# A mixture-of-experts stage: the eighth row block of the gate and up matrices as one fp32 product instead of three split ones

## The chip, the cores and the metric

The kernel runs on one core of a Trainium2 chip. The core's engines work side by side and meet through semaphores: TensorE (PE in the profile, with its weight loads as PEld), VectorE (DVE), ScalarE (ACT), GpSimd (POOL), and SyncE (SP), which here only issues DMA transfers. The metric is the device time of one execution in microseconds (us); the median of several runs counts, and lower is better.

## The reference, cut to what matters

A two-layer encoder on 512 tokens of width 1024, in float32. Each layer has a token mixer (attention of two kinds) and a mixture of experts. Only the experts matter here: a router picks two of 16 experts for each token, and each expert is a SwiGLU block with an inner width of 256.

```python
hg = jnp.einsum('td,edf->tef', t, w_gate)     # w_gate: (16, 1024, 256) per layer
hu = jnp.einsum('td,edf->tef', t, w_up)
act = jax.nn.silu(hg) * hu * combine[..., None].astype(t.dtype)
y = jnp.einsum('tef,efd->td', act, w_down)    # w_down: (16, 256, 1024)
```

`combine` is zero for the experts that a token did not choose, so the kernel computes each expert for its own tokens only.

## The kernel before, in words

**Split products.** A float32 product on PE takes several passes over the moving operand. The kernel replaces most of them by a product of two rounded parts: an operand z is split into H, z rounded to the type fp32r, and L, the rest z - H, also fp32r. Three fp32r matmuls, H·H, H·L and L·H, then stand for one float32 product. ACT writes H (a copy with a change of type) and DVE writes L (a subtraction). `wsplit` (lines 197 to 220; ACT at line 217, DVE at line 218) does this for a weight matrix, in pieces of 512 columns; `split_ps` (lines 341 to 343) for a tile that stands in PSUM; and `gemm3` (lines 222 to 229) issues the three matmuls of each 128-row block k, at lines 227, 228 and 229.

**One expert** (lines 1129 to 1210). At most 128 tokens go to an expert. `x_load` gathers their rows from DRAM into `xe` (line 1133, an indirect DMA issued by POOL). `x_split` transposes the eight 128x128 blocks of `xe` on PE, four at a time into one PSUM tile, and splits them into `xH` and `xL` (lines 342 and 343). `x_prod` splits one weight matrix of 1024x256, held as eight row blocks of 256 columns, in four pieces of two blocks, and multiplies: eight blocks times three matmuls of 256 columns, all added up in one PSUM tile `mm`. `x_gate` does this for the gate matrix and applies SiLU (ACT, line 1159); `x_up` does it for the up matrix, multiplies both results (DVE, line 1166, tile `ea`) and splits a part of the down matrix. `x_down` transposes `ea` to `eT` (ACT, line 1186), and multiplies it with the down matrix at line 1203: of its four blocks of 128 rows and 512 columns, two are split and two go unsplit as float32 products that read the raw tile (group `mm<-raw,eT`). DVE scales the result with a row (`ye`, line 1204), and POOL adds it to `xsum` in DRAM with an indirect DMA (line 1208, a scatter-add). The last two experts of a layer skip the scatter; their results stay in SBUF (`yk`).

**The order.** The loop over experts calls gate(e), down(e-1), up(e) and the split for e+1 in turn. A framework orders the instructions on each engine by priority and by its own estimate of time, and sets the semaphores; each engine then works its list in order. Split pieces go through a ring of six buffers for H and six for L (`NWH = 6`), ten pieces per expert. Raw weights, 1 MB each, go through nine buffers (five `e8` and four `raw`), so a load waits until the matrix three experts earlier is through; those of the first four experts are issued ahead of the stage. All weight loads are issued by SP, in order (line 194 for most).

**The end of a layer.** When the last scatter-add has landed, SP loads `xsum` back (line 1336, `xs`), and behind it the first block of the next layer's `w_in`. PE then adds up `xs` and the two kept experts (lines 1343 and 1360, tile `y`).

**Other tiles that the change touches.** `mhalf` is a constant tile of -0.5, of which `pool_rsqrt` uses up to ten columns. `oc`, `code`, `sh` and `sg` are tiles of `overflow`, a branch for an expert with more than 128 tokens.

```python
H = wp.tile([P, h] + shape[1:], F32R, tag="wH", name="wH", bufs=NWH)
L = wp.tile([P, h] + shape[1:], F32R, tag="wL", name="wL", bufs=NWH)
...
ACT.copy(H, raw(s))
V.tensor_sub(L, raw(s), H.bitcast(F32))
...
PE.matmul(o, lhsT=lH, rhs=rH, start=(i == 0), stop=False)
PE.matmul(o, lhsT=lH, rhs=rL, start=False, stop=False)
PE.matmul(o, lhsT=lL, rhs=rH, start=False, stop=(i == n - 1))
```

The lines of code above are cut from `wsplit` and `gemm3`; the functions follow with their line numbers.

Of the kernel before, what the change touches and what calls it, by code (L numbers as in the profile page):

```python
# [8 lines left out]
F32 = mybir.dt.float32  # L9
F32R = mybir.dt.float32r  # L10
BF16 = mybir.dt.bfloat16
I32 = mybir.dt.int32
# [6 lines left out]
P = 128  # L19
S = 512  # L20
D = 1024
NT = S // P
DEPTH = 2
HD = 64
NE = 16
# [10 lines left out]
def constants():  # L36

    parts = []
    off = [0]

    def add(name, a):
        a = np.asarray(a, np.float32).reshape(P, -1)
        _COLS[name] = (off[0], a.shape[1])
        off[0] += a.shape[1]
        parts.append(a)

    p = np.arange(P)
    add("ident", np.eye(P))
    add("tri", (p[:, None] < p[None, :]))
    row = np.repeat(np.arange(S // 64), 64).astype(np.float32)  # L50
    col = np.tile(np.arange(64), S // 64).astype(np.float32)
    inv = (10000.0 ** (-np.arange(0, 32, 2, dtype=np.float64) / 32)).astype(np.float32)
    ang = np.concatenate([row[:, None] * inv, col[:, None] * inv], -1).astype(np.float64)
    cos = np.repeat(np.cos(ang), 2, axis=-1)
    sin = np.repeat(np.sin(ang), 2, axis=-1)
    sin[:, 0::2] *= -1.0
    add("cos", cos.reshape(NT, P, HD).transpose(1, 0, 2))
    add("sin", sin.reshape(NT, P, HD).transpose(1, 0, 2))
    slope = np.exp2(-8.0 * np.arange(1, 13) / 12).astype(np.float32)

    def bias(g, dist, valid):
        b = -slope[4 * g:4 * g + 4, None, None] * dist[None].astype(np.float32)
        b = np.where(valid[None], b, np.float32(NEG))
        return b[[0, 2, 1, 3]].transpose(1, 0, 2)

    d0 = np.abs(np.arange(256)[None, :] - 64 - p[:, None])
    add("bias0", bias(0, d0, d0 <= 64))
    d1 = np.abs(p[None, :] - p[:, None])
    add("bias1", bias(1, 4 * d1, d1 <= 64))
    add("bias2", bias(2, 4 * d1, d1 % 4 == 0))  # L70
    enc = np.zeros((P, NT, 2))
    for t in range(NT):
        enc[:, t, 0] = 128 * (NT - 1 - t)
        enc[:, t, 1] = 128 - p
    add("enc", enc)
    add("iota", np.tile(p, (P, 1)))
    sel = np.zeros((P, 2, P))
    for i in range(8):
        sel[i, i % 2, (i % 4 // 2) * 64:(i % 4 // 2) * 64 + 64] = 1.0
    add("sel", sel)  # L80
    add("mhalf", np.full((P, 16), -0.5))
    return np.ascontiguousarray(np.concatenate(parts, 1))


def build(tc, A, out):
    nc = tc.nc
    with ExitStack() as es:
# [11 lines left out]
        V, ACT, PE, PO, SY = nc.vector, nc.scalar, nc.tensor, nc.gpsimd, nc.sync  # L99
# [7 lines left out]
        def sc(name, shape, dt=F32, p=P):  # L107
            return sp.tile([p] + list(shape), dt, tag="sc", name=name)

        def small(name, shape, dt=F32, bufs=4, p=P):  # L110
            return sm.tile([p] + list(shape), dt, tag=name, name=name, bufs=bufs)
# [85 lines left out]
        def wsplit(src, shape, big=False, tag="raw", behind=()):  # L197

            raw = src if callable(src) else wraw(src, shape, tag)
            a = shape[0]  # L200
            h = 512 // shape[1] if shape[1] < 512 else 1
            hs = []
            if big:
                h = a // 2
                Hb = e8("wHb", shape, F32R)
                Lb = e8("wLb", shape, F32R)
            for i in range(a // h):
                s = slice(i * h, (i + 1) * h)
                if big:
                    H, L = Hb[:, s], Lb[:, s]  # L210
                else:
                    H = wp.tile([P, h] + shape[1:], F32R, tag="wH", name="wH", bufs=NWH)
                    L = wp.tile([P, h] + shape[1:], F32R, tag="wL", name="wL", bufs=NWH)
                with ExitStack() as order:
                    for z in behind:
                        order.enter_context(tc.issue_after(z.ins))
                    ACT.copy(H, raw(s))  # L217
                    V.tensor_sub(L, raw(s), H.bitcast(F32))  # L218
                hs.append((H, L))
            return lambda k, c: tuple(z[:, k % h, c] for z in hs[k // h])  # L220

        def gemm3(o, ks, lf, rf):
            n = len(ks)
            for i, k in enumerate(ks):
                lH, lL = lf(k)
                rH, rL = rf(k)
                PE.matmul(o, lhsT=lH, rhs=rH, start=(i == 0), stop=False)  # L227
                PE.matmul(o, lhsT=lH, rhs=rL, start=False, stop=False)  # L228
                PE.matmul(o, lhsT=lL, rhs=rH, start=False, stop=(i == n - 1))  # L229

        def row_load(src):
            r = rp.tile([P, D], F32, tag="row", name="row")
# [108 lines left out]
        def split_ps(p, H, L):  # L341
            ACT.copy(H, p)  # L342
            return V.tensor_sub(L, p, H.bitcast(F32))  # L343
# [79 lines left out]
        def layer(l, hH, hL, W0, after=None, qk=None):  # L423
# [586 lines left out]
            def x_src(e, w):  # L1010
                if (e, w) in PRE:
                    return PRE.pop((e, w))
                a = A["w_exp_" + w][l, e]
                return a.rearrange("(k p) n -> p k n", p=P) if w == "down" else a.rearrange("(p k) n -> p k n", p=P)
# [123 lines left out]
            def x_split(e):  # L1138
                xe = XE.pop(e)
                xH = f4("xH", [8, P], F32R)  # L1140
                xL = f4("xL", [8, P], F32R)
                for q in range(2):
                    p = ptp([P, 4, P])
                    transposes(lambda i: xe[:, (4 * q + i) * P:(4 * q + i + 1) * P], p, 4)
                    i = split_ps(p, xH[:, 4 * q:4 * q + 4, :], xL[:, 4 * q:4 * q + 4, :])
                XS[e] = xH, xL
                return i

            def x_prod(e, w):
                xH, xL = XS[e]  # L1150
                W = wsplit(x_src(e, w), x_shape(w), tag=tags.get((e, w)), behind=[order1] if (e, w) in BEHIND else [])
                p = pmm([P, 256])
                gemm3(p, range(8), lambda k: (xH[:, k, :], xL[:, k, :]), lambda k: W(k, slice(0, 256)))
                return p

            def x_gate(e):
# [70 lines left out]
            def overflow():  # L1227
# [3 lines left out]
                with tc.If(rv > CAP):  # L1231
                    token_weights()
                    row = rt("row", [2, NT])
                    V.tensor_scalar(row, sv[:, 0], float(CAP), None, op0=OP.is_ge)
                    code = rt("code", [NT])
                    V.tensor_add(code, enc[:, :, 0], enc[:, :, 1])
                    ow = sc("ow", [2, NT, NE])
                    V.tensor_mul(ow, tmp, row[:, :, :, None].to_broadcast([P, 2, NT, NE]))
                    V.tensor_mul(row, row, code[:, None].to_broadcast([P, 2, NT]))
                    oc = sc("oc", [2, NT, NE])  # L1240
                    V.tensor_mul(oc, o12, row[:, :, :, None].to_broadcast([P, 2, NT, NE]))
                    V.tensor_add(oc[:, 0], oc[:, 0], oc[:, 1])
                    oi = sc("oi", [NE * NT], I32)
                    V.tensor_scalar(oi.rearrange("p (e t) -> p t e", t=NT), oc[:, 0], -1.0, float(S), op0=OP.mult, op1=OP.add)
                    og = sc("og", [NE * NT])
                    V.tensor_add(og.rearrange("p (e t) -> p t e", t=NT), ow[:, 0], ow[:, 1])
                    sh = sc("sh", [NE * NT], I32)
                    sg = rt("sg", [NE * NT])
                    with tc.For_i(0, NE, 1) as e:
                        def blocks(w, tags, view):  # L1250
                            r = []
# [177 lines left out]
```

## Time and profile before

| What | Value |
|---|---|
| Median of three runs | 1363.2 us (1360.3 to 1363.39) |
| Profiled execution, its own time | 1365.39 us |
| Span in its trace | 1363.6 us |
| PE busy, share of the span | 1269.8 us, 93% |
| DVE busy | 1015.7 us, 74% |
| ACT busy | 712.3 us, 52% |
| Granted TensorE clock, mean | 0.975 of full speed |
| DMA moved | 259.37 MB, mean 190 GB/s |

The experts' stage of layer 0 lies at about 500 to 675 us of the span, that of layer 1 at about 1162 to 1336 us. A group of instructions in the profile is named by its line, its engine and its tiles (out<-in); "x512" is a count, and two times behind a bar are the sum of busy time in us and the mean of one in ns. Matmuls are pipelined: the recorded duration of one is longer than the distance to the next, so what a matmul costs in a row of them is the distance between starts. The idle time in brackets is that of the engine just before the instruction, with what ended it.

### The profile page before, as it was taken

How to read it: one execution, taken by the hardware profiler on the slowest of the kernel's cores; microseconds unless marked ns; L12 is line 12 of the kernel's file. 1: busy time of each engine (PE TensorE's matmuls, PEld its weight loads, DVE VectorE, ACT ScalarE, POOL GpSimd, SP SyncE). 2: the span in 40 equal slices, each digit the busy share in tenths (PEclk: the TensorE clock that was granted, in tenths of full speed). 3: DMA queues.
4: the chain of work that ended last, by engine and by line, in shares of the span. 5: the costliest groups of instructions: out<-in, count | busy, mean ns of one | idle time of the engine just before them, and what ended most of it. 6: DMA issues, size and time to landing. Idle time of an engine off the chain costs nothing.

```text
span 1363.6 us, 21396 instructions
## 1 busy us (share of the span) xinstructions
PE 1269.8 (93%) x7967; PEld 1031.1 (76%) x7971; DVE 1015.7 (74%) x2064; ACT 712.3 (52%) x1476; POOL 145.5 (11%) x122
## 2 busy tenths in 40 slices
PE   5899999999999959999889999999999995899997
PEld 4788777778778948888658777777777795788883
DVE  5888778766378879999587887564235878799986
ACT  2344444554744157777445445456555513777770
POOL 1031000000000012222111300000000001223210
PEclk9999999999999969999989999999999997999999
DMA  9745555346165178999553455121214534889963
GB/s 319 230 140 169 185 186 184 126 155 210 38 201 217 63 276 327 313 342 330 177 186 129 155 186 186 63 62 63 63 47 141 192 131 171 322 300 352 335 187 153
DMA packets 124221, 259.37 MB, mean 190 GB/s; under 512 B 18009, under 2 KB 67577, under 8 KB 116176
## 3 DMA queue, kind: packets, MB, share of 16 engines
q1 hardware_dynamic: 102672, 225.46, 46.6%
q0 software_dynamic: 9184, 15.69, 4.9%
q10 hardware_dynamic: 12256, 16.80, 3.9%
q8 instruction: 64, 1.05, 0.3%
q14 instruction: 45, 0.37, 0.1%
HBM read 246.57 MB, written 27.30 MB: 201 GB/s over the span
## 4 chain that ended last, share of the span: by engine, by line
PE 39%; DVE 14%; ACT 4%; DMA 3%; issue 3%; POOL 1%; SPq 0%; ACTq 0%; POOLq 0%; DVEq 0%
DVE wL L218 8%; PE mm L229 6%; PE mm L228 6%; PE mm L227 6%; PE mm L1203 6%; PE tp L335 3%; PE y L1343 2%; PE av L664 1%; ACT wH L217 1%; DMA xr<-xdr 1%; PE y L1360 1%; DMA raw<-in_w_in 1%; ACT eT L1186 1%; DMA xe<-h2d,tidx 1%; DVE ea L1166 1%
## 5 line engine op out<-in xcount | busy, mean ns | idle before, releaser
L218 DVE TENSOR_TENSOR wL<-raw,wH 128x512 fp32r<-128x512 f32 x520 | 340.4, 686 | 95.5 <-ACT wH L217 85.1
L217 ACT CAST wH<-raw 128x512 fp32r<-128x512 f32 x520 | 318.8, 622 | 159.6 <-PE mm L1203 45.7
L227 PE MATMUL mm<-hH,wH 128*128 128x512 f32 x544 | 218.8, 402 | 0.0
L228 PE MATMUL mm<-hL,wH 128*128 128x512 f32 x544 | 216.9, 399 | 0.0
L229 PE MATMUL mm<-hH,wL 128*128 128x512 f32 x544 | 215.8, 397 | 0.0
L227 PE MATMUL mm<-wH,xH 128*128 128x256 f32 x512 | 148.0, 289 | 0.5 <-ACT xH L342 0.5
L229 PE MATMUL mm<-wH,xL 128*128 128x256 f32 x512 | 147.0, 288 | 0.5 <-DVE xL L343 0.5
L228 PE MATMUL mm<-wL,xH 128*128 128x256 f32 x512 | 145.7, 285 | 0.5 <-DVE wL L218 0.5
L228 PEld LDWEIGHTS mm<-hL,wH 128*128 128x128 f32 x544 | 103.0, 189 | 21.6 <-issue 1.8
L227 PEld LDWEIGHTS mm<-hH,wH 128*128 128x128 f32 x544 | 103.0, 189 | 21.5 <-issue 0.8
L229 PEld LDWEIGHTS mm<-hH,wL 128*128 128x128 f32 x544 | 103.0, 189 | 21.2 <-issue 0.7
L251 DVE SCALAR_TENSOR_TENSOR acc<-araw,cond,acc 128x512 f32<-128x512 f32 x148 | 110.6, 748 | 4.7 <-DMA araw<-in_w_ada 1.9
L227 PEld LDWEIGHTS mm<-wH,xH 128*128 128x128 f32 x512 | 98.1, 192 | 2.6 <-ACT xH L342 1.4
L228 PEld LDWEIGHTS mm<-wL,xH 128*128 128x128 f32 x512 | 98.1, 192 | 2.1 <-DVE wL L218 0.9
L229 PEld LDWEIGHTS mm<-wH,xL 128*128 128x128 f32 x512 | 97.4, 191 | 1.4 <-DVE xL L343 0.9
L1208 POOL DMA_INDIRECT xsum<-ye,tidx x28 | 50.4, 1800 | 214.8 <-DVE wL L218 116.8
L288 POOL TENSOR_TENSOR rstd<-rstd,c_mhalf 128x1 f32<-128x1 f32 x32 | 19.6, 614 | 490.0 <-DVE rstd L287 475.3
L638 ACT ACTIVATE pp<-s,nm,rs 128x512 f32<-128x512 f32 x64 | 49.7, 778 | 33.3 <-DVE nm L635 30.9
L1203 PE MATMUL mm<-raw,eT 128*128 128x512 f32 x128 | 63.3, 617 | 3.7 <-ACT eT L1186 1.6
L227 PE MATMUL mm<-wH,hH 128*128 128x256 f32 x192 | 56.9, 299 | 7.1 <-ACT hH L407 4.3
L229 PE MATMUL mm<-wH,hL 128*128 128x256 f32 x192 | 55.4, 295 | 1.9 <-DVE hL L377 0.9
L228 PE MATMUL mm<-wL,hH 128*128 128x256 f32 x192 | 55.0, 290 | 0.0
(299 smaller groups left out, 2637.6 us busy)
## 6 DMA issues: line engine op xcount, KB each, us to landing
araw<-in_w_ada SPq DMA_DIRECT2D x44, 1024.0 KB
raw<-in_w_in SPq DMA_DIRECT2D x40, 1024.0 KB
raw<-in_w_exp_gate SPq DMA_DIRECT2D x32, 1024.0 KB
raw<-in_w_exp_up SPq DMA_DIRECT2D x30, 1024.0 KB
raw<-in_w_exp_down SPq DMA_DIRECT2D x28, 1024.0 KB
raw<-in_w_out SPq DMA_DIRECT2D x8, 1024.0 KB
eraw<-in_w_ada SPq DMA_DIRECT2D x4, 1024.0 KB
raw<-in_w_branch_a SPq DMA_DIRECT2D x4, 1024.0 KB
```

Source lines behind the costliest of these rows:

```text
L217: ACT.copy(H, raw(s))
L218: V.tensor_sub(L, raw(s), H.bitcast(F32))
L227: PE.matmul(o, lhsT=lH, rhs=rH, start=(i == 0), stop=False)
L228: PE.matmul(o, lhsT=lH, rhs=rL, start=False, stop=False)
L229: PE.matmul(o, lhsT=lL, rhs=rH, start=False, stop=(i == n - 1))
L251: last = V.scalar_tensor_tensor(acc, raw[:, k, :], ck, acc, op0=OP.mult, op1=OP.add)
L288: PO.tensor_tensor(r, r, mhalf[:, :n], op=OP.pow)
L335: return PE.transpose(dst, src, ident[0:k, 0:k])
L638: ACT.activation(pp, s, AF.Exp, bias=nm, scale=rs, accum_out=dn)
L1203: PE.matmul(p, lhsT=a, rhs=w, start=(i == 0), stop=(i == len(todo) - 1))
L1208: PO.indirect_dma_start(out=xsum, out_offset=bass.IndirectOffsetOnAxis(ap=tidx[:, e:e + 1], axis=0), in_=ye, in_offset=None, bounds_check= ...
L1343: PE.matmul(Y[t][j], lhsT=G[:, i, t, :], rhs=YE[i][:, 512 * j:512 * j + 512], start=start, stop=stop)
```

## The change

In each gate and up product, the eighth row block of the weights is no longer split. The first six blocks are split in three pieces of two blocks, the seventh in a piece of its own, and for the eighth PE takes one float32 product of the raw weights with `xF`, an unsplit float32 copy of the eighth block of the transposed tokens, which ACT makes from PSUM. `xH` and `xL` get seven blocks. `gemm3` leaves the sum open (`stop=False`) for that last product. The tile `xF` takes 512 bytes per partition, twice; `mhalf` shrinks from 16 to 10 columns, and tiles of the overflow branch share memory.

```diff
-            h = 512 // shape[1] if shape[1] < 512 else 1
+            h = min(a, 512 // shape[1]) if shape[1] < 512 else 1
...
-        def gemm3(o, ks, lf, rf):
+        def gemm3(o, ks, lf, rf, stop=True):
...
-                PE.matmul(o, lhsT=lL, rhs=rH, start=False, stop=(i == n - 1))
+                PE.matmul(o, lhsT=lL, rhs=rH, start=False, stop=stop and i == n - 1)
...
-                    i = split_ps(p, xH[:, 4 * q:4 * q + 4, :], xL[:, 4 * q:4 * q + 4, :])
-                XS[e] = xH, xL
+                    n = 4 * q + (3 if q else 4)
+                    i = split_ps(p[:, 0:n - 4 * q], xH[:, 4 * q:n, :], xL[:, 4 * q:n, :])
+                    if q:
+                        xF = small("xF", [P], bufs=2)
+                        ACT.copy(xF, p[:, 3])
+                XS[e] = xH, xL, xF
...
-                xH, xL = XS[e]
-                W = wsplit(x_src(e, w), x_shape(w), tag=tags.get((e, w)), behind=[order1] if (e, w) in BEHIND else [])
+                xH, xL, xF = XS[e]
+                raw = x_src(e, w)
+                if not callable(raw):
+                    raw = wraw(raw, x_shape(w), tags[e, w])
+                behind = [order1] if (e, w) in BEHIND else []
+                W6 = wsplit(raw, [6, 256], behind=behind)
+                W1 = wsplit(lambda s: raw(slice(6, 7)), [1, 256], behind=behind)
                 p = pmm([P, 256])
-                gemm3(p, range(8), lambda k: (xH[:, k, :], xL[:, k, :]), lambda k: W(k, slice(0, 256)))
+                gemm3(p, range(7), lambda k: (xH[:, k, :], xL[:, k, :]),
+                      lambda k: W6(k, slice(0, 256)) if k < 6 else W1(0, slice(0, 256)), stop=False)
+                PE.matmul(p, lhsT=xF, rhs=raw(slice(7, 8))[:, 0], start=False, stop=True)
                 return p
...
-    add("mhalf", np.full((P, 16), -0.5))
+    add("mhalf", np.full((P, 10), -0.5))
...
-                    code = rt("code", [NT])
+                    oc = sc("oc", [2, NT, NE])
+                    code = oc[:, 0, :, 0]
...
-                    oc = sc("oc", [2, NT, NE])
...
-                    sh = sc("sh", [NE * NT], I32)
-                    sg = rt("sg", [NE * NT])
+                    sh = sc("sh", [2, NE * NT], I32)
+                    sh, sg = sh[:, 0], sh[:, 1].bitcast(F32)
```

## Rows read from the trace of the kernel before

**Rows 1.** The page: busy time of each engine, and the chain by line.

```profile
PE 1269.8 (93%) x7967; PEld 1031.1 (76%) x7971; DVE 1015.7 (74%) x2064; ACT 712.3 (52%) x1476; POOL 145.5 (11%) x122
...
DVE wL L218 8%; PE mm L229 6%; PE mm L228 6%; PE mm L227 6%; PE mm L1203 6%; PE tp L335 3%; PE y L1343 2%; PE av L664 1%; ACT wH L217 1%; DMA xr<-xdr 1%; PE y L1360 1%; DMA raw<-in_w_in 1%; ACT eT L1186 1%; DMA xe<-h2d,tidx 1%; DVE ea L1166 1%
```

**Rows 2.** Windows, two experts of layer 0: length, busy per engine, PEclk, DMA share, GB/s.

```profile
558.85:569.20 10.35, 10.27 (x71) 8.81 (x69) 9.54 (x17) 8.02 (x17) 3.12 (x2) 1.00 0.98 320
600.28:610.65 10.37, 10.29 (x71) 8.81 (x69) 9.55 (x17) 8.01 (x16) 2.69 (x2) 1.00 0.96 348
```

**Rows 3.** The chain of waits, one expert of layer 0: start, length, what.

```profile
590.34 2.69 PE mm L1203 x7
...
598.37 1.90 DVE wL L218 x3
```

**Rows 4.** Timeline of PE: first matmul of an up product, transposes behind it.

```profile
593.54 0.28 PE L227 MATMUL mm<-wH,xH 128*128 128x256 f32 x1
...
596.42 0.60 PE L335 MATMUL tp<-c_ident,xe 128*128 128x128 f32 x4
```

**Rows 5.** Timeline of PE's weight loads: the down product, and block 4 of gate.

```profile
600.70 0.30 PEld L1203 LDWEIGHTS mm<-raw,eT 128*128 128x128 f32 x2 [0.32 <-ACT eT L1186]
601.24 0.19 PEld L1203 LDWEIGHTS mm<-raw,eT 128*128 128x128 f32 x1 [0.24 <-issue]
601.67 0.19 PEld L1203 LDWEIGHTS mm<-raw,eT 128*128 128x128 f32 x1 [0.24 <-issue]
...
608.65 0.19 PEld L228 LDWEIGHTS mm<-wL,xH 128*128 128x128 f32 x1
608.87 0.19 PEld L229 LDWEIGHTS mm<-wH,xL 128*128 128x128 f32 x1
```

**Rows 6.** Groups by line over the whole span, the same shapes kept apart.

```profile
L218 DVE TENSOR_TENSOR wL<-raw,wH 128x512 fp32r<-128x512 f32 x520 | 340.4, 686 | 95.5 <-ACT wH L217 85.1 <-PE tp L335 3.8 <-PE pa L228 1.7
...
L229 PE MATMUL mm<-wH,xL 128*128 128x256 f32 x512 | 147.0, 288 | 0.5 <-DVE xL L343 0.5
...
L664 PE MATMUL av<-pT,vA 128*64 128x256 f32 x256 | 41.6, 389 | 0.0
...
L343 DVE TENSOR_TENSOR eL<-tp,eH 128x256 fp32r<-128x256 f32 x32 | 13.6, 425 | 6.3 <-ACT eH L342 3.7
...
L342 ACT CAST eH<-tp 128x256 fp32r<-128x256 f32 x32 | 12.5, 391 | 0.0
```

**Rows 7.** Timelines of DVE and ACT: second `xL` of an expert; `wH` behind L1203.

```profile
608.12 0.69 DVE L343 TENSOR_TENSOR xL<-tp,xH 128x512 fp32r<-128x512 f32 x1
...
603.42 4.19 ACT L217 CAST wH<-raw 128x512 fp32r<-128x512 f32 x6 [1.49 <-PE mm L1203]
```

**Rows 8.** Timeline of PE, among the first experts of layer 0.

```profile
523.76 0.28 PE L227 MATMUL mm<-wH,xH 128*128 128x256 f32 x1
...
525.13 0.39 PE L228 MATMUL mm<-wL,xH 128*128 128x256 f32 x1 [0.24 <-DVE wL L218]
```

**Rows 9.** SP's queue, layer 0: its waits (total, times, longest) and two issues.

```profile
SPq L194 <- DVE wL L218: 108.8, 23, 11.7
...
591.82 0.34 SPq L194 DMA_DIRECT2D raw<-in_w_exp_gate  x1
...
633.83 0.33 SPq L194 DMA_DIRECT2D raw<-in_w_exp_up  x1
```

**Rows 10.** POOL's last scatters of layer 0, and the chain behind them.

```profile
642.59 1.59 POOL L1208 DMA_INDIRECT xsum<-ye,tidx  x1 [7.83 <-DVE wL L218]
653.57 1.88 POOL L1208 DMA_INDIRECT xsum<-ye,tidx  x1 [9.39 <-DVE eL L343]
660.66 2.02 POOL L1208 DMA_INDIRECT xsum<-ye,tidx  x1 [5.21 <-DVE xL L343]
...
660.66 6.71 DMA xsum<-ye,tidx
...
669.70 11.13 DMA raw<-in_w_in
```

## The prediction

> **What bounds the kernel now.** I read the profile's page first. TensorE (PE) is busy 93% of the span, VectorE (DVE) 74%, and the chain that ended last names line 218, DVE's `wL`, as its largest single group [rows 1]. Both engines could therefore be the limit, and the change takes from one what it gives to the other, so the question is settled in the stage it touches: the 16 experts of each layer. There, in the middle of the stage, PE is busy 10.27 of 10.35 us, DVE 9.54, ScalarE (ACT) 8.02, and the DMA engines have a share of 0.98 [rows 2]. Four resources stand close together. The reader should not take the 99% of PE as proof, since ends of matmuls are modelled.
>
> The chain of waits comes next. Its pieces repeat every 10.36 us per expert: L1203 starts at 590.34 and its next weight load at 600.70 [rows 3, 5]. Through most of a period it runs over DVE's `wL` (1.90 us for three) and then ACT's `eT`. That looks like DVE as the bound. But a chain shows one of several equal paths, so I looked at whether PE really stands still. Its order in a period is: down of the expert before, up, four transposes, gate, transposes, down. The up product's first matmul starts at 593.54 and the transposes behind its last at 596.42 [rows 4]: 24 matmuls in 2.88 us, 0.12 us each, without a gap. In the weight loads, whose starts are not modelled, two places are open [rows 5]. The load ahead of L1203 waits 0.32 us for ACT's `eT`; and the load of `xL` in block 4 of the gate product comes 0.22 us behind the one before it (608.65 to 608.87) where the pitch is 0.12, so 0.10 is lost. The second is DVE's: the `xL` of that half ends at 608.12 + 0.69 = 608.81 [rows 7]. The first is no queue at all: `eT` follows the SiLU on ACT, and that follows the gate product's end; it is PE to ACT to PE. So of 10.36 us some 9.94 are PE's own work, 0.32 is a turn-round that a lighter DVE doesn't touch, and 0.10 is DVE. **PE is the bound; DVE runs just behind it.**
>
> **The change, part by part.** *Three matmuls become one fp32 product, in each of 64 gate and up products.* Removed: 3 x 0.12 = 0.36 us [rows 4]. Added: no row has a 128x256 fp32 product with 128 weight columns. Every fp32 product in the trace is two instructions (the `raw` group of L1203 has four for two products), and at 512 columns their loads follow each other by 0.43 us (601.24 to 601.67) [rows 5]. Half the columns give 0.215 each, 0.43 for the product. A second way agrees: one fp32 instruction of 256 columns lasts 389 ns in L664 against 288 for a 256-column one of the split kind [rows 6], 0.10 longer, so 0.12 + 0.10 = 0.22. I take 0.43: +0.07 per product, 64 x 0.07 = **+4.6 us** (64 x 0.072). Upper end: the split matmuls need 0.12 for what their 512-column pitch would make 0.107, a surcharge of 0.013; with it each instruction costs 0.227, +0.094 per product, +6.0. A lower price is excluded by the two rows that agree.
>
> Here a rule can be set against the rows. The Trainium skill, "TensorE: Matmul & The Clock Gate", section Back-to-back issue gap, gives columns/2.4 GHz plus 2.5 ns for a warm matmul, 109 ns for 256 columns, and "FP8 and Floating Point Precision", section TensorE Precision Notes, gives true FP32 four passes; by these three split passes take 0.33 us, the fp32 product 0.44, and the term would be +7 instead of +4.6. The trace's 0.12 is above the first figure and 2 x 0.215 agrees with the second; I keep the rows.
>
> *DVE and ACT get less.* The last split piece shrinks from 512 to 256 columns: on DVE from 686 to about 425 ns, on ACT to about 391 [rows 6], twice per expert; the second `xL` goes from four to three blocks (half of 686 - 425, 0.13). ACT gains the copy `xF` of 128 columns, at most 0.39 by its 256-column row, less than its two shorter pieces save. On DVE that is 2 x 0.26 + 0.13 = 0.65 us per expert. Most of it is worth nothing, since PE covers it, and ACT already waits 1.49 us per expert for L1203 to free a slot [rows 7]. What it buys is the 0.10 in block 4: `xL` would end 0.13 sooner, before its load is due. There are some 27 such periods (16 experts less the first two and half of the last, twice): 27 x 0.10 = **-2.7 us** (ends 0 and -2.7).
>
> *First experts.* There DVE does hold PE: two neighbouring matmuls of one product start at 523.76 and 525.13, the second behind `wL` [rows 8], as DVE also makes the kept experts' weights. Of these 1.37 us, 0.12 is the matmul and a part is transposes that are due anyway, so at most 1.25 a layer is there to gain. DVE has one shorter piece and a shorter `xL` ahead of this point, 0.26 + 0.13: I take 0.4 for each layer, **-0.8** (ends 0 and -2.5).
>
> *The raw tile is held longer.* PE now reads it at the very end of the product. SP's loads mostly wait for `wL` [rows 9]; the gate load at 591.82 would instead wait until the up product is through, 596.42 [rows 4], 4.6 us later, and whatever stands behind it on SP's queue with it. The weights themselves have cover: the last up load leaves at 633.83 [rows 9], more than 26 us before its use, since expert 15's up product comes after expert 13's scatter (660.66) [rows 10]. If that cover were gone, ACT's `wH` would wait for a load by what is missing.
>
> *The scatters are late next.* Each scatter-add to `xsum` follows the one before. Under the load of weights they came 10.98 us apart (642.59 to 653.57), without it 7.09 (to 660.66), and the last one of layer 0 leads through `xs` into the `w_in` load that is on the chain until 680.83 [rows 10]. Weights that arrive 4.6 us later reach further into these scatters. Ends: 0, and 10.98 - 7.09 = 3.9 for one more scatter under load. The nearer row is the 7.09, that of the last scatter itself, which the loads are unlikely to reach; a quarter of the way to the other end is **+1.0**.
>
> *The rest*: `mhalf` is narrower by columns that nothing reads, and `oc`, `sh`, `sg` move inside the branch for overflow, which doesn't run; 0 us.
>
> Sum: 4.6 - 2.7 - 0.8 + 1.0 = +2.1 us. The profiled execution took 1365.39 us (span 1363.6), 2.2 above the median 1363.2 of the three runs. 1365.39 + 2.1 = 1367.5 in its terms, and **1365.3** against the median. A difference under 0.3% (4.1 us) can't be told from none, so this is "same", on the slower side.
>
> **Rivals.** *DVE sets the period (faster).* For it: the chain names `wL` first [rows 1, 3], and 9.54 of 10.35 us with semaphores between leaves little. Then both waits of PE close, the period falls to PE's work, 9.94 + 0.14 = 10.08, 27 x 0.28 = 7.6 us go, and 0.8 at the first experts: 1363.2 - 8.4 = 1354.8. Against it: only 0.10 us of PE's waiting ends with DVE.
>
> *Late weights push the scatters (slower).* Place: experts 11 to 13 of layer 0. It decides when the last gate and up loads, now out by 633.83, slip past the scatter of 653.57's start and that scatter takes 11.0 instead of 7.1: +3.9, passed on whole to the `w_in` load, in place of my 1.0; with half of that again where layer 1 reads `xs`, 1363.2 + 1.1 + 3.9 + 2 = 1370.2. For it: a DMA share of 0.98 and an order by which SP holds everything behind a late slot. Against it: the share has room once the last loads are out.
>
> *Another order.* The framework orders instructions by its own estimate of time; a moved transpose or copy could cost or give 0.2 us in each of 27 periods, 5 us, either way.
>
> **How the numbers follow.** My forecast gets 0.50, DVE as the bound 0.23, late weights 0.22, another order 0.05. The forecast's own bounds are 1363.2 + 4.6 - 2.7 - 2.5 = 1362.6 and 1363.2 + 6.0 + 3.9 = 1373. The range reaches down to the DVE rival's 1355 and up to 1371, past the late-weights case. Faster by over 0.3% (under 1359.1): the DVE rival's 0.23 and 0.02 of another order, 0.25. Slower (over 1367.3): 0.08 of the forecast's upper part, 0.20, 0.02: 0.30. The rest, 0.45, is the same.
>
> **What would show it.** Right: a period of 10.4 to 10.5 us; two weight loads of `xF` 0.21 apart with nothing idle between; the block-4 gap gone; the 0.32 ahead of L1203 still there; DVE's busy share in the stage down by six points with no gain in time; raw loads issued behind PE instead of `wL`. Wrong: a period under 10.3, or `eT` earlier (DVE did matter); an fp32 pair above 0.5 us; `wH` waiting for a DMA; the last scatter of layer 0 more than 4 us later than L1203 of its expert explains.

## The result and the profile after

The changed kernel took 1370.4 us (median of 4 runs, 1369.2 to 1371.3), the kernel before 1362.3 in the runs beside them (4 runs, 1360.3 to 1363.4): a ratio of 1.0057, 95% interval 1.003 to 1.0084. Measured again later with more runs of each it was 1368.7 (12 runs) against 1363.2 (35 runs), 1.0031 with 1.0009 to 1.0053. By these ratios the change costs 4 to 8 us, where the sum gave 2.1. Both medians lie in the range given, but past 1367.3, the line from which the prediction called the kernel slower (with a chance of 0.30, against 0.45 for the same).

One profiled execution of each is not enough to see where: the first traces differ by 4.4 us in span (1368.0 to 1363.6), and a second trace of the kernel before has 1361.8. So the stages of the experts are compared over two traces of each kernel.

The page of the changed kernel, its busy times and its chain by line, in answer to [rows 1]:

```profile
PE 1268.3 (93%) x7907; PEld 1023.8 (75%) x7907; DVE 995.9 (73%) x2064; ACT 697.4 (51%) x1508; POOL 146.4 (11%) x122
...
PE 12%; ACT 1%; DVE 1%; issue 0%; ACTq 0%; DVEq 0%
PE mm L1214 4%; PE mm L229 2%; PE mm L227 2%; PE mm L228 2%; PE y L1354 1%; ACT wH L217 1%; PE mm L1164 1%; PE tp L335 1%; PE y L1371 1%; ACT eT L1197 0%; ACT ea L1170 0%; DVE wL L218 0%; PE gp L1119 0%; DVE xo L317 0%; DVE xo L323 0%
```

This chain reaches back only to the start of layer 1's stage (its shares add up to 14% of the span), that of the kernel before to 495 us, so the two can't be compared as they stand. Over the same stretch, from 1161 us to the end, DVE's `wL` has 27.8% of the chain before and 1.3% now: it is as good as gone, and the kernel is slower all the same. The windows of two experts, in answer to [rows 2]:

```profile
561.88:572.38 10.50, 10.33 (x66) 8.69 (x66) 8.92 (x17) 7.52 (x17) 3.57 (x2) 1.00 0.94 318
...
593.38:603.88 10.50, 10.33 (x66) 8.69 (x66) 8.92 (x17) 7.52 (x17) 2.44 (x2) 1.00 1.00 342
```

DVE's busy time fell by 0.62 us per expert and ACT's by 0.5, yet the period rose from 10.36 to 10.50. PE's weight loads show its parts, in answer to [rows 5] (block 4 of one gate product, then the end of a gate product two experts later):

```profile
569.89 0.19 PEld L228 LDWEIGHTS mm<-wL,xH 128*128 128x128 f32 x1
570.01 0.19 PEld L229 LDWEIGHTS mm<-wH,xL 128*128 128x128 f32 x1
...
591.85 0.31 PEld L1164 LDWEIGHTS mm<-raw,xF 128*128 128x128 f32 x2
592.18 0.36 PEld L335 LDWEIGHTS tp<-c_ident,ea 128*128 128x128 f32 x2
592.51 0.47 PEld L335 LDWEIGHTS tp<-c_ident,xe 128*128 128x128 f32 x4
593.38 0.30 PEld L1214 LDWEIGHTS mm<-raw,eT 128*128 128x128 f32 x2 [0.41 <-ACT eT L1197]
...
603.88 0.30 PEld L1214 LDWEIGHTS mm<-raw,eT 128*128 128x128 f32 x2 [0.41 <-ACT eT L1197]
```

The gap in block 4 is closed (0.12 where it was 0.22). But the wait ahead of the down product, 0.32 before, is now 0.41. Two products at 0.072 more, less 0.10, plus 0.09, make the 0.135 by which the period grew. Why the wait grew is seen on ACT. First the timeline of the changed kernel, then that of the kernel before at the same place of a period:

```profile
590.90 0.26 ACT L1149 COPY xF<-tp 128x128 f32<-128x128 f32 x1
591.14 1.65 ACT L217 CAST wH<-raw 128x512 fp32r<-128x512 f32 x3
592.69 0.38 ACT L1170 ACTIVATE ea<-mm 128x256 f32<-128x256 f32 x1
592.97 0.36 ACT L1197 COPY eT<-tp 128x256 f32<-128x256 f32 x1
```

```profile
588.92 0.62 ACT L217 CAST wH<-raw 128x512 fp32r<-128x512 f32 x1 [0.17 <-PE mm L229]
589.63 0.38 ACT L1159 ACTIVATE ea<-mm 128x256 f32<-128x256 f32 x1
589.91 0.37 ACT L1186 COPY eT<-tp 128x256 f32<-128x256 f32 x1
```

Before, ACT was through with `wH` at 589.54 and began the SiLU at 589.63, when the gate product allowed it. Now three `wH` stand ahead of it without a pause, and the SiLU starts in their tail: 0.13 us behind the end of the gate product's last matmul (an end that the profile models) where it was 0.03. From the SiLU's start to the first weight load of the down product it is 0.7 us in both kernels, so the wait grew ahead of the SiLU. The chain of waits of the changed kernel (layer 1: start, length, what) says the same:

```profile
1314.12 0.43 PE mm L1164 x2
1314.55 0.44 PE tp L335 x4
...
1317.22 0.31 ACT wH L217
...
1317.75 0.40 ACT wH L217
1318.15 0.28 ACT ea L1170
1318.43 0.27 ACT eT L1197
```

The fp32 pair is the predicted 0.43, and the way into the down product now leads through ACT's `wH` where it led through the gate product's end.

**The first experts.** From the first down product to the second it is 11.56 us in both layers where it was 12.06 to 12.09, a gain of 0.5. The start of a stage gave it back. Weight loads of the second expert's gate product, changed kernel:

```profile
515.02 0.19 PEld L229 LDWEIGHTS mm<-wH,xL 128*128 128x128 f32 x1 [0.97 <-DVE xL L343]
```

and kernel before:

```profile
512.45 0.19 PEld L229 LDWEIGHTS mm<-wH,xL 128*128 128x128 f32 x1 [0.43 <-DVE xL L343]
```

On DVE two `wL` (1.28 us from 513.08) now stand ahead of that `xL` at 514.28, where one stood.

**The end of layer 0's stage** hangs on the scatters, and I had not seen how much. The timeline of POOL, SP and PE's weight loads, changed kernel:

```profile
658.41 1.57 POOL L1219 DMA_INDIRECT xsum<-ye,tidx  x1 [9.27 <-DMA xsum<-ye,tidx]
665.20 1.55 POOL L1219 DMA_INDIRECT xsum<-ye,tidx  x1 [5.22 <-DVE wL L218]
...
671.41 2.02 SPq L1347 DMA_DIRECT2D xs<-xsum  x4
673.61 11.01 SPq L194 DMA_DIRECT2D raw<-in_w_in  x4
...
686.68 0.50 PEld L1354 LDWEIGHTS y<-yk,G 128*128 128x128 f32 x2 [7.55 <-DVE yk L1215]
```

and SP's waits there (total, times, longest):

```profile
SPq L1347 <- DMA xsum<-ye,tidx: 23.1, 1, 23.1
```

In the kernel before PE's wait is there too, here with what ACT and DVE do ahead of it:

```profile
680.86 0.62 ACT L217 CAST wH<-raw 128x512 fp32r<-128x512 f32 x1 [9.94 <-DMA raw<-in_w_in]
681.51 0.69 DVE L218 TENSOR_TENSOR wL<-raw,wH 128x512 fp32r<-128x512 f32 x1 [7.96 <-ACT wH L217]
682.12 0.68 DVE L1204 TENSOR_TENSOR yk<-mm,row 128x512 f32<-128x512 f32 x1
682.86 0.50 PEld L1343 LDWEIGHTS y<-yk,G 128*128 128x128 f32 x2 [6.91 <-DVE yk L1204]
```

SP stands 23 us at the load of `xs` until the last scatter has landed, and the loads of the next layer's `w_in` stand behind it on the same queue. ACT waits for them, and DVE waits for ACT's `wH`. The `yk` that PE needs stands behind that `wL` in DVE's queue, so PE stands still for 7 us in the combine. So in layer 0 the stage ends when the last scatter lets it, in layer 1, where no `w_in` follows, when PE is through. The times, from the starts of the first transposes of `xe`, the first down product, that of expert 13, the last scatter and the last combine product in four traces (us after the first transposes; "scatter" is the last scatter behind expert 13's down product):

```
                 layer 0: down 0  down 13  scatter  end      layer 1: down 0  end
before, 1st trace         15.9     152.4    +8.1    205.8             16.0    192.4
before, 2nd trace         16.8     153.2    +6.9    204.9             16.0    192.3
changed, 1st trace        17.4     155.0    +8.8    208.2             16.8    194.5
changed, 2nd trace        17.4     155.1    +9.5    208.9             16.6    194.3
```

By the means, layer 0 costs 3.2 us more and layer 1 2.1. Together that is 5.3, close to the difference of the larger set of runs (1368.7 - 1363.2 = 5.5). The 3.2 is the less certain: two executions of one kernel differ by 0.9 in layer 0, and the last kernel below, which has the order of the kernel before in layer 0, took 203.6 there.

The weights are issued later, as expected, because the raw tile is held until PE has read it. SP's last up load of layer 0, in answer to [rows 9]:

```profile
641.72 0.33 SPq L194 DMA_DIRECT2D raw<-in_w_exp_up  x1
```

That is 140.3 us behind the first transposes, where it was 133.6, and still early enough: ACT waits for no expert's weights longer than 0.6 us.

### The profile page after: what moved, and what is told of

Read it like the earlier page. It is cut to its first block, busy times and chain, and to the rows that moved or that the text cites. A ratio compares the mean times of both kernels' runs of the same rounds, so it can differ in the third digit from the quotient of the medians.

```text
span 1368.0 us, 21393 instructions
## 1 busy us (share of the span) xinstructions
PE 1268.3 (93%) x7907; PEld 1023.8 (75%) x7907; DVE 995.9 (73%) x2064; ACT 697.4 (51%) x1508; POOL 146.4 (11%) x122
## 3 DMA queue, kind: packets, MB, share of 16 engines
q10 hardware_dynamic: 12256, 16.80, 3.8%
q8 instruction: 64, 1.05, 0.3%
## 5 line engine op out<-in xcount | busy, mean ns | idle before, releaser
L218 DVE TENSOR_TENSOR wL<-raw,wH 128x512 fp32r<-128x512 f32 (+1 forms) x520 | 326.2, 654 | 101.2 <-ACT wH L217 90.2
L217 ACT CAST wH<-raw 128x512 fp32r<-128x512 f32 (+1 forms) x520 | 298.1, 593 | 170.6 <-PE mm L1214 61.1
L227 PE MATMUL mm<-wH,xH 128*128 128x256 f32 x448 | 130.8, 292 | 0.7 <-ACT xH L342 0.7
L229 PE MATMUL mm<-wH,xL 128*128 128x256 f32 x448 | 127.9, 285 | 1.5 <-DVE xL L343 1.5
L228 PE MATMUL mm<-wL,xH 128*128 128x256 f32 x448 | 127.9, 285 | 0.0
L227 PEld LDWEIGHTS mm<-wH,xH 128*128 128x128 f32 x448 | 86.9, 194 | 2.8 <-ACT xH L342 1.6
L229 PEld LDWEIGHTS mm<-wH,xL 128*128 128x128 f32 x448 | 86.5, 193 | 1.9 <-DVE xL L343 1.9
L228 PEld LDWEIGHTS mm<-wL,xH 128*128 128x128 f32 x448 | 87.0, 194 | 1.2
L1215 DVE TENSOR_TENSOR ye<-mm,row 128x512 f32<-128x512 f32 x56 | 38.5, 688 | 35.1 <-PE mm L1214 34.9
```

The costliest lines, as they stand in the source:

```text
L229: PE.matmul(o, lhsT=lL, rhs=rH, start=False, stop=stop and i == n - 1)
L1215: V.tensor_mul(ye[:, js], p, r_g2[:, js])
```

## The experiments

**The kernel before, again**, unchanged, for its second trace.

> The kernel before, unchanged, for a second trace of it: how far do two executions of one kernel differ? Theory (the stage of the experts costs more): the period of an expert in the middle of a stage is again 10.36 us to within 0.01, the start of a stage (first transposes of xe to the first down product) again 15.9 to 16.0 us in both layers. Rival (the traces differ by chance, and 1.5 us more at the start of layer 0 is the clock's phase): the start of the stages differs by 0.5 us or more between the two traces of the kernel before.

Measured: 10.34 to 10.38 us per expert; the stages began in 16.80 and 16.00 us. So the period can be relied on to 0.02, but the start of layer 0 moves by 0.9 between two executions of one kernel. Of the 1.05 by which it is longer in the changed kernel, only the 0.54 of `xL` and 0.08 of `eT` that stand in both layers of both its traces are counted as the change's.

**The fp32 product on half of its columns**, put between the sixth and the seventh row block:

```diff
-PE.matmul(p, lhsT=xF, rhs=raw(slice(7, 8))[:, 0], start=False, stop=True)
+gemm3(p, range(6), ..., stop=False)
+PE.matmul(p[:, 0:128], lhsT=xF, rhs=raw(slice(7, 8))[:, 0, 0:128], start=False, stop=False)
+gemm3(p, [6], ..., start=False)
```

> The changed kernel with the fp32 product on 128 of its 256 columns only (leaves out the eighth row block for half of the output columns; loads, split pieces and all other work stay). Theory, PE is the bound: each of the 64 products is 0.215 us shorter on PE, the period falls from 10.50 to about 10.07, and the kernel takes 12 to 14 us less than the changed one, 1356 to 1358 us, some 5 below the kernel before. Rival, DVE or ACT sets the period: PE only waits longer ahead of the down product or of a block, the period stays at 10.4 or more and the time within 4 us of the changed kernel.

Measured: 1368.2 us, ratio to the kernel before 1.0044 (1.0024 to 1.0064), period 10.43. By its number that speaks for the rival, and at this point my reading of PE as the bound seemed to fall. The weight loads at the end of a gate product tell why it says less than it should:

```profile
608.44 0.24 PEld L335 LDWEIGHTS tp<-c_ident,ea 128*128 128x128 f32 x2
608.82 0.30 PEld L1164 LDWEIGHTS mm<-raw,xF 128*128 128x128 f32 x2
609.03 0.19 PEld L227 LDWEIGHTS mm<-wH,xH 128*128 128x128 f32 x1
...
609.40 0.46 PEld L335 LDWEIGHTS tp<-c_ident,xe 128*128 128x128 f32 x4
610.40 0.30 PEld L1215 LDWEIGHTS mm<-raw,eT 128*128 128x128 f32 x2 [0.54 <-ACT eT L1198]
```

The fp32 product costs 0.21 here, half of 0.43, as it should. But the framework moved `ea`'s two transposes ahead of it, and those had covered a part of ACT's turn-round: the wait grew to 0.54. From the up product's start to the transposes behind it 0.2 us were saved; behind them the order gave it back. Undecided: the edit had changed two things.

**The turn-round closed, first try**: `ea`'s transposes, `eT`, `eH`, `eL` go into the middle of the next gate product, in the changed kernel and in the kernel before.

```diff
-p = x_prod(e, "gate")
+p = x_prod(e, "gate", (lambda: x_turn(e - 1)) if e > 0 else None)  # after 4 blocks
...
-def x_down(e):
+def x_turn(e):
```

> The changed kernel with ea's two transposes, eT, eH and eL of an expert moved into the middle of the next expert's gate product, so that PE has something to do while ACT makes SiLU and eT. Theory, the 0.41 us ahead of the down product is a turn-round from PE through ACT (wH, SiLU, eT) to PE: it closes, 27 periods of 10.50 become 10.1, and the kernel takes 1359 to 1362 us, 9 to 11 us less than the changed one. Rival, the wait is the slack of another engine's cycle (DVE's or ACT's 10.4 us): PE waits elsewhere by as much, the period stays above 10.4 and the time within 3 us.

> The same move in the kernel before. Theory, PE is the bound and 0.32 us of its period is the turn-round: the period falls from 10.36 to 10.05, the time by 7 to 9 us to 1354 to 1356, and the changed kernel with the move (about 1360) is slower than this one by the fp32 products' 4.6 us. Rival, DVE runs so close behind (9.54 of 10.35 us busy) that it takes over: the period stays at 10.2 to 10.36, PE waits for wL or xL in the gate product, and this kernel gains less than the changed one does from the same move.

Measured: 1377.6 us (ratio 1.0103, 1.0078 to 1.0129) and 1370.4 us (1.0059, 1.004 to 1.0078), periods 11.07 and 11.0. Both theories missed. The kernel before with the move, PE's weight loads:

```profile
599.96 0.90 PEld L335 LDWEIGHTS tp<-c_ident,xe 128*128 128x128 f32 x8
601.42 0.19 PEld L227 LDWEIGHTS mm<-wH,xH 128*128 128x128 f32 x1 [0.56 <-ACT xH L342]
602.14 0.19 PEld L229 LDWEIGHTS mm<-wH,xL 128*128 128x128 f32 x1 [0.43 <-DVE xL L343]
```

The wait ahead of the down product is gone, but with nothing to fill there the framework no longer put four of `xe`'s transposes in that place. All eight came together ahead of the gate product, which then waited 0.56 and 0.43 us for `xH` and `xL`: a new wait of 1.0 for one of 0.32.

**The turn-round closed, the order kept.** The same, with the first four transposes written out between gate and down product, the others behind the up product:

```diff
 x_gate(e)
+if e + 1 < NE: x_split(e + 1, (0,))
 if e > 0: x_down(e - 1)
 x_up(e)
-if e + 1 < NE: x_split(e + 1)
+if e + 1 < NE: x_split(e + 1, (1,))
```

> The kernel before with ea's transposes, eT, eH and eL in the middle of the next gate product, as in the run before, and with the four transposes of the next xe kept between the gate product and the down product, and the other four behind the up product, where the kernel before has them (the run before had all eight together ahead of the gate product, and PE waited there for xH and xL, 1.0 us). Theory, PE is the bound and 0.32 of its 10.36 us is the turn-round by ACT: the period falls to 10.0 to 10.1, the time by 7 to 9 us to 1354 to 1357. Rival, DVE or ACT takes over: the period stays above 10.25 and PE waits for wL or xL.

> The same for the changed kernel. Theory, PE is the bound: the 0.41 us close, the period falls from 10.50 to about 10.1, the time by 9 to 11 us to 1359 to 1361, and it stays 3 to 5 us above the kernel before with the same order (64 fp32 products at 0.072 us more). Rival, with the turn-round closed DVE is the bound: then this kernel, whose DVE has 0.65 us less to do for each expert, is the faster of the two, by up to 8 us.

Measured: 1364.4 us for the kernel before with this order (ratio 1.0003, 0.9978 to 1.0029), 1367.2 for the changed one (1.0027, 1.0005 to 1.0048). The windows of one expert, kernel before with this order:

```profile
598.56:608.49 9.93, 9.93 (x70) 8.70 (x69) 9.27 (x17) 7.90 (x16) 2.48 (x2) 1.00 0.96 352
```

and the changed kernel with it:

```profile
597.18:607.26 10.08, 10.08 (x69) 8.66 (x68) 8.93 (x17) 7.42 (x17) 2.62 (x2) 1.00 0.99 353
```

This settles the middle of the stage. With its waits gone PE runs at 9.93, the 9.94 read as "PE's own work"; DVE, at 9.27, does not take over. In the changed kernel periods of 10.08 and 10.06 follow each other, 10.07 in the mean: 0.135 more per expert, two fp32 products at 0.07. But 0.43 us in each of some 26 periods, 11 us, did not come through in the whole. In layer 1 the stage took 187.6 us where it was 192.3, in layer 0 205.8 as before (the changed kernel with this order: 193.2 and 205.9). And the traced execution took 1360.2 us, 4.2 under the median of its 12 runs, so not every execution won even the 4.7 of layer 1. What became late there, ACT's timeline in layer 0:

```profile
634.42 2.70 ACT L217 CAST wH<-raw 128x512 fp32r<-128x512 f32 x5 [4.77 <-DMA raw<-in_w_exp_down]
```

A load of an expert's weights comes 4.8 us late and makes one period 14.19, where the four traces of the two kernels have no such wait of ACT over 0.6; and the last scatter leaves 140.8 us after the first as it did before (140.2 and 138.9), though PE's other periods are shorter.

**The changed kernel, again**, with more runs.

> The changed kernel, unchanged, for a second trace of it and more times beside the kernels of this call. Theory (0.135 us more in each of 26 periods, some 3.5 us, and 1 to 2 us in the scatters): again 10.50 us per expert, 4 to 8 us above the kernel before. Whether the start of a layer's stage also costs more: it took 17.4 and 16.75 us in the first trace of this kernel, 15.9 to 16.8 in two traces of the kernel before; if it is a cost of the change it is above 16.7 here too in both layers, if it is chance it is 16.2 or less in one of them.

Measured: 1368.7 us (ratio 1.0031), 10.50 us per expert again (10.55 once), the stages begun in 17.42 and 16.59 us. By the rule written down the start is neither clearly the change's nor chance; the 0.97 at `xL` is there in both layers. The granted clock separates the two. Layer 0's first transposes run at 0.5, and the clock is back at 1.0 3.1 and 5.2 us after them in the two traces of the kernel before, 5.2 and 5.4 in those of the changed one. In the kernels with half of the scatters (below) it is the other way round, 5.4 in the kernel before and 3.0 in the changed one, and so are the starts, 16.9 and 16.4 us. Where the clock is back at like times, the change costs 0.5 (16.4 to 15.9) to 0.6 us (17.4 to 16.8) at the start of layer 0; the rest of the 1.05 goes with the clock.

**The copy `xF` on DVE** in place of ACT.

```diff
-ACT.copy(xF, p[:, 3])
+V.tensor_copy(xF, p[:, 3])
```

> The changed kernel with the copy xF made by DVE instead of ACT. In the first trace ACT runs wH, xF, three wH and the SiLU without a pause, so the SiLU may be late by its queue. Theory A, the 0.09 us by which the wait ahead of the down product grew is ACT's queue, to which the 0.26 us of xF belongs: the wait falls from 0.41 to 0.32 or less, the period from 10.50 to 10.41, 2 to 3 us go. Theory B, the SiLU waits for the gate product's end alone, which is later on PE by the length of the last fp32 instruction: the wait and the period stay within 0.02 us.

Measured: 1370.9 us (ratio 1.0042, 1.0022 to 1.0062), period 10.47.

```profile
592.61 2.37 ACT L217 CAST wH<-raw 128x512 fp32r<-128x512 f32 x4 [0.23 <-PE mm L229]
594.88 0.37 ACT L1170 ACTIVATE ea<-mm 128x256 f32<-128x256 f32 x1
...
595.57 0.30 PEld L1214 LDWEIGHTS mm<-raw,eT 128*128 128x128 f32 x2 [0.35 <-ACT eT L1197]
```

The wait falls from 0.41 to 0.35, so two thirds of its growth were `xF` in ACT's queue, as theory A has it. The last third isn't separated: `wH` still ends only as the SiLU starts, and the gate product still ends with an fp32 instruction. The period falls by only 0.03, a third of what A expected, and the first experts (11.72 for 11.56) lose some of it again. The time shows no gain.

**Half of the scatters**, in the kernel before, in the changed one, and in the kernel before with the kept order:

```diff
+if e % 2:
+    return
 PO.indirect_dma_start(out=xsum, ...)
```

> The kernel before without the scatter-adds of the odd experts 1 to 13 (leaves out their rows of xsum; all products stay). In layer 0 the scatters follow each other 10.8 us apart whatever PE's period is (9.93, 10.36 or 10.50), and the end of the stage lies 44.3 to 45.3 us behind the last scatter. Theory, the scatters set the end of layer 0's stage and PE that of layer 1's: with half of them layer 0's stage ends as layer 1's does, by PE: from the first transposes of xe to the last combine product 4 us or more less than the 205.3 of the kernel before, and layer 1 stays at 192.3 within 1 us. Rival, the scatters only run beside PE: both layers stay within 1 us.

> The same for the changed kernel. Layer 0's stage cost 3.2 us more than in the kernel before (208.5 to 205.3), layer 1's 2.1 (194.4 to 192.3). Theory: with half of the scatters PE alone decides, and both layers cost 1.8 to 2.3 us more than in the kernel before with half of them (13 periods at 0.135 and 0.3 at the first experts). Rival, the extra of layer 0 is from somewhere else than the scatters: it stays at 3 us or more.

> The kernel before with ea's transposes in the middle of the gate product and the order of the run that had a period of 9.93, again without the scatter-adds of the odd experts. With all scatters that order gained 4.7 us in layer 1 and nothing in layer 0, though its periods were 0.43 shorter in both. Theory, layer 0's gain was given back to the scatters and to one load of weights that came 4.8 us late beside them: with half of the scatters layer 0 gains 4 us or more on the kernel before with half of them, as layer 1 does. Rival, the weights' loads alone set layer 0 (3 MB for each expert): the load still comes late and layer 0 gains less than 2 us.

Measured: 1359.0 us (ratio 0.9962, 0.9944 to 0.9979), 1359.3 (0.9983, 0.9962 to 1.0004) and 1342.4 (0.9866, 0.9823 to 0.991). The stages took 202.3 and 192.5 us, 200.6 and 194.5, 192.3 and 186.4 (layers 0 and 1). In SP's waits of the first of these the 23 us are 9:

```profile
SPq L1338 <- DMA xsum<-ye,tidx: 8.8, 1, 8.8
```

and PE's wait of 7 us in the combine is gone. Still, layer 0 of the kernel before gained 3.0 us and not the 4 expected. Three things follow. Layer 1 costs 2.1 us more in the changed kernel with half of the scatters as with all, so that part is PE's. Layer 0's 3.2 us are gone with the scatters, and more than that: the stage is 1.75 shorter, not 1.8 to 2.3 longer as I had expected. PE's part is there (1.45 us more from the first to the last down product), the start is 0.5 shorter, with the clock back earlier, and behind the last down product's start the kernel before needs 30.9 us and the changed one 28.2. Another load now sets the end: DVE waits 2.4 us in the one and 1.4 in the other for `row<-in_ln_g` and `row<-in_ln_b`, PE waits for `hn` behind it (4.28 and 3.29 us), and the transposes of `hn` begin 192.1 us after the first of `xe` in both, so that PE's 1.45 is hidden. The last 1.7 us lie behind `hn`, among combine products that stand between products of layer 1; they were not followed further. And the kept order, worth nothing in layer 0 with all scatters, is worth 10.0 us there with half of them (1.5 of it in the start of the stage). The rival in which the weights' loads alone hold layer 0 falls: with half of the scatters every period in the middle was 9.93 and no load of an expert came late. Whether the scatters hold the stage by their own pace or also by slowing the loads beside them isn't separated, as leaving half of them out frees both.

**The kept order in layer 1 alone**, nothing left out, as the version that might beat both:

```diff
-x_prod(e, "gate", (lambda: x_turn(e - 1)) if e > 0 else None)
+x_prod(e, "gate", (lambda: x_turn(e - 1)) if l and e > 0 else None)
```

> The kernel before with that order in layer 1 alone, where the scatters have slack; nothing is left out. Theory: layer 1's stage takes 187.6 us instead of 192.3, layer 0 stays as it was, and the kernel takes 4 to 5 us less than the kernel before, 1358 to 1360, 9 less than the changed one. Rival, layer 1's end then meets its scatters too, as in the changed kernel with that order (y's products 29.2 us instead of 23.5): within 1.5 us of the kernel before.

Measured: 1360.8 us (12 runs, 1356.8 to 1369.1) against 1364.6, ratio 0.9981 (0.9957 to 1.0005): not clearly faster than the kernel before. In its trace layer 1 took 193.7 us, not 187.6. This time a load came late in layer 1 too,

```profile
1293.78 3.22 ACT L217 CAST wH<-raw 128x512 fp32r<-128x512 f32 x6 [4.00 <-DMA raw<-in_w_exp_down]
```

and the combine waited for the scatters, the last of which left 11.2 us behind its expert instead of 7.6. So the trace looks as the rival has it. But the traced execution took 1365.6, 4.7 above the median, and the median, 3.8 under that of the kernel before, is nearer to the theory: the runs don't decide, and how often a load comes late is not known. By the medians it is 8 us under the changed kernel (1368.7), but the two were not timed side by side.

## Why the prediction was right or wrong

The time lies in the range and on the forecast's side of the kernel before, and PE as the bound is borne out. But the sum gave 2.1 us and 5.3 to 5.5 came, because neither of the two gains that DVE's relief was to bring reached the time. That the range holds the result is in part luck: its upper end was drawn for a rival whose cause isn't there.

**The fp32 products, +4.6: right.** The pair takes 0.43 us in the chain (its weight loads lie 0.12 apart, not 0.21 as the signs had it), and where nothing else holds PE the two products of an expert cost 0.135 more (10.07 to 9.93), 64 x 0.067 = 4.3. An estimate from the Trainium skill ("TensorE: Matmul & The Clock Gate", Back-to-back issue gap, with the four passes of "FP8 and Floating Point Precision", TensorE Precision Notes) made it +7, 0.22 per expert; the rows and the 0.135 decide against that.

**PE as the bound in the middle of a stage: right**, as shown by the 9.93, and with it that the relief of DVE is worth little. The rival "DVE sets the period" fell: it had both of PE's waits close and a period of 10.08, and one closed while the other grew. (A period of 10.07 came only when PE was given other work in that wait.)

**The gap in block 4, -2.7: the step that failed.** The gap did close. But the text had the turn-round ahead of the down product as "no queue at all", a fixed 0.32 that a lighter DVE doesn't touch. It is fixed only while ACT is free when the gate product ends. The same edit that shortened DVE's pieces moved ACT's: the copy `xF` and three `wH` now run up to the SiLU, and the wait grew by 0.09. Over 26 periods that gives 2.3 of the 2.7 back. ACT was counted by its busy time, which fell, and not by what stands in its queue ahead of the one instruction that PE waits for.

**The first experts, -0.8: wrong.** The 0.5 per layer at that point came true (12.08 to 11.56), and 0.62 was lost before it, 0.54 of it at one `xL` behind two `wL`: +0.1 per layer, not -0.4. Again the order of a queue, not its length.

**The scatters, +1.0: right in size, by luck.** The last one of layer 0 leaves 1.6 us later behind its expert (means of 9.1 and 7.5), and 0.6 comes back behind it. But the term was to come from later weights that put one more scatter under load, and that did not happen: the last scatter follows the one before by 6.8 and 7.0 us, where it was 7.1. What made the scatters later is open. With the terms so corrected the sum is 4.3 - 2.7 + 2.3 + 0.2 + 1.0 = 5.1, near what was measured (5.3 in the stages, 5.5 in the runs); but the corrections are read from these same traces, and about half a microsecond of the 5.3 goes with the clock at the start of layer 0.

**The raw tile, 0: right.** Among layer 0's experts SP's loads now wait for PE's transposes (66.4 us in 21 waits) where they waited for `wL` (86.3 in 20), the last up load leaves 6.7 us later behind the first transposes, and the cover holds.

**"Late weights push the scatters"** gave 1370.2, near the measured time, by a cause that isn't there: the loads leave later, but none is late for ACT, and the last scatter was not slowed. But it named the right place. Layer 0's stage ends by its scatters, in the kernel before too: PE's 6.9 us of waiting in the combine were in its trace, and the prediction read only the chain behind the last scatter. What the half-scatter kernels leave open is how the 3.2 us of layer 0 split between PE's later products and the scatters' own pace, since with half of them another load sets its end.

## What to carry to other kernels

When work moves between engines, ask of each queue what will stand ahead of the one instruction that the bounding engine waits for; a lower busy share says nothing of that. A wait that looks like a fixed latency of an engine pair should be checked for how long the second engine was idle just before: here 0.09 us, and that was all the room there was. And before closing such a wait, look for the next limits: here loads and scatters stood so close behind PE that a wait of 0.43 us, closed in some 26 periods, gave nothing in the median time.

## What was not expected of the hardware

The scatter-adds of layer 0 took 138.9 to 142.4 us from the first to the last of 14 in the two kernels and in both with the kept order, at expert periods from 9.93 to 10.50: 10.7 to 11.0 us apart on average, the last two 7 us in every one of them, when the loads of weights are through. (With half of the fp32 columns, at 10.43, they took 144.3.)

An fp32 product of 128 columns costs 0.21 to 0.23 us where one of 256 columns costs 0.43: down to there its price goes by columns.

Two executions of the kernel before differ by 0.9 us in the start of layer 0's stage. PE comes to it at a granted clock of 0.5, the lower level of 1.2 GHz, after 20 us in which it was busy for 6 (480 to 500 us of the kernel before). In the windows of the kernel before, and below them those of the changed one,

```profile
500.00:503.00 3.00, 2.81 (x13) 2.62 (x14) 1.43 (x3) 1.61 (x4) 0.29 (x2) 0.50 0.82 280
503.00:506.00 3.00, 3.00 (x26) 3.00 (x26) 2.57 (x9) 2.69 (x5) 0.89 (x1) 0.95 1.04 418
```

```profile
503.00:506.00 3.00, 3.00 (x15) 2.82 (x14) 2.13 (x7) 2.34 (x5) 0.99 (x1) 0.50 0.84 304
506.00:509.00 3.00, 3.00 (x24) 2.95 (x24) 2.01 (x4) 1.93 (x4) 0.00 (x0) 0.89 1.00 330
```

the full clock (1.0, 2.4 GHz) is back some 3 us later in the second (506.7 for 503.3), which begins its transposes only 1.2 us later. A difference of under 1 us in a stage that begins so says nothing from one trace.
